# A macaron step on one core: the second product's sevenfold order starts with a one-block product, and stores follow their sums by a step

## The chip, the cores and the metric

The kernel runs on one core of a Trainium2 chip. The metric is the device time of one execution in microseconds. Its engines are TensorE (PE in the profile, with its weight loads as PEld), VectorE (DVE), ScalarE (ACT), GpSimd (POOL) and the sync engine (SP), which here issues all transfers (DMA). Each engine works through its own queue in program order; semaphores tie the queues together.

## The reference

One layer of a decoder: a half-step SwiGLU feed-forward block, a token mixer (a causal pooling branch and a Mamba-2 SSD branch under sigmoid gates), a second half-step feed-forward block, and a final norm, over 1024 prompt tokens and 64 sample tokens, in float32. The change touches the feed-forward blocks, in `after1` and `turn_x` the first one alone:

```python
D_MODEL = 1024; D_FF = 2816

def rmsnorm(x, g):
    return x * rsqrt(mean(x * x, -1) + EPS) * g

def swiglu(x, w_in, w_out):
    gu = x @ w_in
    g, u = gu[..., :D_FF], gu[..., D_FF:]
    return (silu(g) * u) @ w_out

x = x + 0.5 * swiglu(rmsnorm(x, norm_ffn1), ffn1_w_in, ffn1_w_out)
x = x + token_mixing(rmsnorm(x, norm_mix), ...)
x = x + 0.5 * swiglu(rmsnorm(x, norm_ffn2), ffn2_w_in, ffn2_w_out)
y = rmsnorm(x, norm_final)
```

## The kernel before

**Stages.** The first feed-forward block takes about 0 to 838 us of the span, the mixer 838 to 2190, the second feed-forward block 2190 to 2959. Activations lie features by tokens, in blocks of 128 features; the tokens are cut into halves of 512 and 576 (the second half has the 64 sample tokens).

**Precision.** Each matrix operand is split into a high and a low part, and each product takes three matmuls: high by high, high by low, low by high. ScalarE makes the high part (a copy that rounds), VectorE or GpSimd the low part by subtraction. For weights these are `wh` and `wl`, for the operands of the second product `hh` and `hr`.

**The first product of a block** makes the 22 hidden blocks of 128 (`ff` = 0 to 21). It, too, goes mostly by seven block products instead of eight (`wino`). A finished hidden block goes to `produced`. Two hidden blocks and two halves of the tokens (even and odd block, "e" and "o"; first and second half, 0 and 1) are the four quarters from which the second product by sevens takes its operands. There are 11 such pairs, `kk` = 0 to 10. The operands of products "2" and "5" are quarters as they stand, and `produced` stores them; those of "6", "7", "1", "4" and "3" are sums or differences, which `sums(kk)` makes on GpSimd and stores to device memory (`xq`), five stores of 128 x 544 per pair, one right behind each sum. The tiles come from one pool, `fx`, of 17 buffers, which the evictions of the first product, the input copy and the split of later weights use as well.

**The second product**, `second()`, runs seven products in the order of `ORDER2`. Each goes through two passes (`m0` = 0 and 2: four output tiles at a time, in four PSUM banks) of six groups of up to two pairs `kk`, 24 matmuls to a full group, 264 to a product. `second_weights` loads the weight blocks of a group (256 KB each) into one of six raw buffers; where the product has two blocks in `BLOCKS2`, GpSimd adds or subtracts them into `ws`; ScalarE then makes `wh`, VectorE `wl`. Products "3" and "4" have one block and need no sum. `fetch_x` loads the next product's 11 operands back ahead of time and splits them: the low part is made by GpSimd for "3" and "6" (`LO_POOL`), by VectorE for the others. For the products in `IN_PAIRS` the operands lie in a set of pair buffers that would be free otherwise. The residual (what is added to) is loaded by `residual` during the first product, and after each pass `add` accumulates the PSUM banks into it with VectorE. When the first half of the tokens has had its last contribution, `after(0, ...)` runs; for the first block that is `after1`, which starts the mixer's norm (`norm_parts`, a chain that makes one of 8 feature blocks, splits it and spills it at each step) and stores the residual back (`xspill`).

**What sets the order.** The instructions are emitted by a program with a clock of its own (`pe`), which each matmul advances by its ideal time. Side work is written as chains; a chain that yields a number is due again that many us of this clock later, and `tick()`, between groups of matmuls, steps the chains that are due. So `yield 4.0` between a load and its use puts about 4 us of matmuls between them in every queue. The order so written is the order of each engine's queue, SP's included: a store that waits for its sum holds every transfer behind it.

**The input copy.** In the first block a chain, `turn_x`, makes a transposed copy of the input for the residual: it loads 18 blocks of it (`xin`), yields, transposes each on TensorE (`ptr`), copies the results out of PSUM and stores them to `xspill`. Another chain, `part`, loads weights of later products, splits them (`ph`) and stores the parts.

Lines of the profile that are spoken of: 175 is every matmul, 179 every transpose; 321 to 328 load and store the parts, 367 and 369 split them; 455 and 456 split the first product's weights; 573, 577 and 579, 601, 609 and 613 evict it; 649 stores the operand of "5"; 672 to 687 are `sums` (674, 684 and 687 its stores); 738 to 749 `second_weights`; 764 to 766 `fetch_x`; 774 `residual`; 784 `add`; 900 the load of the input copy; 920 the norm.

Of the kernel before, what the change touches and what calls it, by code (L numbers as in the profile page):

```python
# [12 lines left out]
ALU = mybir.AluOpType  # L13
# [32 lines left out]
STEP_S = 1.0  # L46
POST, RIPE = 1.0, 3.0
GP = (1.5, 1.2)
HN_AT, HN_PACE = 3.0, 2.0
MP = 2.0  # L50
R_WAIT0 = 3.5
R_WAIT = 0.5
# [5 lines left out]
SETS = (((0,), (1,), (2,), (3,)), ((0, 1), (2,), (3,)))  # L58
PART_AT, PART_W, PART_PACE = 20.0, 4.0, 3.0
NKK, NQ, NA = NFF // 2, 272, 32  # L60
ORDER2 = "2517436"
BLOCKS2 = {"1": ((0, 0), (1, 1)), "2": ((0, 1), (1, 1)), "3": ((0, 0),), "4": ((1, 1),), "5": ((0, 0), (1, 0)),
           "6": ((0, 1), (0, 0)), "7": ((1, 0), (1, 1))}
MINUS2 = "67"
INTO2 = {"1": ((0, 0, 1), (1, 1, 1)), "2": ((1, 0, 1), (1, 1, -1)), "3": ((0, 1, 1), (1, 1, 1)),
         "4": ((0, 0, 1), (1, 0, 1)), "5": ((0, 0, -1), (0, 1, 1)), "6": ((1, 1, 1),), "7": ((0, 0, 1),)}
IN_PAIRS = "214"
LO_POOL = "36"
X_AT, X_PACE = 5.0, 2.2
SUM_PACE = 1.5  # L70
# [3 lines left out]
def tile_hybrid_pool_ssd_macaron(  # L74
# [88 lines left out]
    def finish(c):  # L163
        while not c.done:
            c.step()
# [491 lines left out]
    def sums(kk):  # L657

        t = {}
        for i in range(2):  # L660
            for h in HALVES:
                g = made.pop((2 * kk + i, h))
                if g is None:
                    g = fx(name="gr")
                    dma(g[:, : NTOK[h]], hdram[h][2 * kk + i])
                    yield 2.0
                t[i, h] = g
        e0, e1, o0, o1 = t[0, 0], t[0, 1], t[1, 0], t[1, 1]
        a, s, b0, b1, n = slice(0, 512), slice(512, 512 + NA), slice(NA, NA + 512), slice(NA + 512, 2 * NA + 512), 2 * NQ

        def both(p, out, x0, x1, y, op):
            G.tensor_tensor(out[:, a], x0[:, a], y[:, b0], op=op)  # L672
            G.tensor_tensor(out[:, s], x1[:, :NA], y[:, b1], op=op)
            dma(xq[p][kk], out[:, :n])

        both("6", fx(name="s6"), e0, e1, e1, ALU.add)
        yield SUM_PACE
        both("7", fx(name="s7"), o0, o1, o1, ALU.add)
        yield SUM_PACE
        both("1", fx(name="s1"), e0, e1, o1, ALU.add)  # L680
        yield SUM_PACE
        G.tensor_tensor(o0[:, a], o0[:, a], e0[:, a], op=ALU.subtract)
        G.tensor_tensor(o0[:, s], o1[:, :NA], e1[:, :NA], op=ALU.subtract)
        dma(xq["4"][kk], o0[:, :n])
        yield SUM_PACE
        G.tensor_tensor(e1[:, NA : NA + n], e1[:, NA : NA + n], o1[:, NA : NA + n], op=ALU.subtract)
        dma(xq["3"][kk], e1[:, NA : NA + n])

    def operands(prep, plain):

# [61 lines left out]
    def second(wo, after, half):  # L752

        X, C = {p: [] for p in ORDER2}, {}
        n = 2 * NQ

        def fetch_x(p, kks, pace):
            for kk in kks:
                if p in IN_PAIRS and kk < N_PAIR:
                    a, t, _ = pair(576, "hp")  # L760
                    t = t.bitcast(F32)
                else:
                    t, a = act((P, 576), F32, "hr"), act((P, 576), F32R, "hh")
                dma(t[:, :n], xq[p][kk])
                S.activation(a[:, :n], t[:, :n], AF.Identity)  # L765
                (G if p in LO_POOL else V).tensor_tensor(t[:, :n].bitcast(F32R), t[:, :n], a[:, :n].bitcast(F32), op=ALU.subtract)  # L766
                X[p].append((a, t.bitcast(F32R)))
                yield pace

        def residual(ms):  # L770
            for m in ms:
                for h in HALVES:
                    C[m, h] = fx(name="x")
                    dma(C[m, h][:, : NTOK[h]], xspill[h][m])
                yield 1.0

        def add(pt, m, side, c, sign):
            if side:
                to = [(1, NA + NQ * c, 0, NQ)]
            else:  # L780
                to = [(0, 0, 0, NQ)] if c == 0 else [(0, NQ, 0, NQ - NA), (1, 0, NQ - NA, NA)]
            for h, at, of, w in to:
                o = C[m, h][:, at : at + w]
                V.scalar_tensor_tensor(o, pt[:, of : of + w], 0.5 * sign, o, op0=ALU.mult, op1=ALU.add)  # L784

        finish(start(fetch_x(ORDER2[0], range(NKK - 1), 0.0)))
        ahead = start(fetch_x(ORDER2[0], range(NKK - 1, NKK), 0.0))
        for at, p in enumerate(ORDER2):
            finish(ahead)
            if at + 1 < len(ORDER2):  # L790
                last = at + 2 == len(ORDER2)
                ahead = start(fetch_x(ORDER2[at + 1], range(NKK), 1.6 if last else X_PACE), 14.0 if last else X_AT)
            for m0 in (0, 2):
                pts = [[psum("pd", "po") for _ in range(2)] for _ in range(2)]
                for kp in range(0, NKK, 2):
                    n2 = min(2, NKK - kp)
                    W2 = second_weights(wo, p, kp, n2, m0)
                    for j in range(2):
                        for k in range(n2):
                            xh, xl = X[p][kp + k]  # L800
                            for i, (w, x) in enumerate(((0, xh), (0, xl), (1, xh))):
                                for c in range(2):
                                    mm(pts[j][c][:, :NQ], W2[w][:, k, j * P : (j + 1) * P], x[:, c * NQ : (c + 1) * NQ],
                                       start=kp + k == 0 and i == 0, stop=kp + k == NKK - 1 and i == 2)
                            tick()
                    if at == 0 and kp == 2:
                        while summing:
                            finish(summing.pop())
                        res = start(residual(range(4, KD) if m0 == 0 else range(4)))
                if at == 0:  # L810
                    finish(res)
                with tc.high_priority(HP_EV):
                    for j in range(2):
                        for c in range(2):
                            for y, side, sign in INTO2[p]:
                                add(pts[j][c], 4 * y + m0 + j, side, c, sign)
            if p == "4":
                after(0, [C[m, 0] for m in range(KD)])
            if p == "3" and half:
                half(1, [C[m, 1] for m in range(KD)])  # L820
        after(1, [C[m, 1] for m in range(KD)])
# [72 lines left out]
    def turn_x(h):  # L894

        for q in range(2):
            x = [fx(name="xr") for _ in range(4)]
            for src, c0, c in blocks_of(h):
                t = fx(name="xin2")
                dma(t[:c, :512], src[:, q * 512 : (q + 1) * 512])  # L900
                yield 4.0
                pt = psum("ps", "ptr")
                for k in range(4):
                    tr(pt[:, k * P : k * P + c], t[:c, k * P : (k + 1) * P], ident[:c, :c])
# [6 lines left out]
    def norm_parts(xt, h, gi, out, pace=1.0, away=None):  # L911
# [5 lines left out]
        for k in range(KD):  # L917
# [5 lines left out]
            lo.append(b)  # L923
            xn.append(x)
            hl.append(both)
            if away:
                dma(away[k], x[:, :N])
            yield pace
        out.append((h, hi, lo, xn, hl))

    wi1 = ffn1_w_in[0]
# [2 lines left out]
    def after1(h, xt):  # L934
        o = []
        if h == 0:
            prep1m[0] = start(norm_parts(xt, 0, i_gm, o, HN_PACE, xnd), HN_AT), o
        for m in range(KD):
            dma(xspill[h][m], xt[m][:, : NTOK[h]])
        if h == 1:  # L940
            finish(prep1m[0][0])
            _, hi, lo, _, hl = prep1m[0][1][0]
# [963 lines left out]
```

## Time and profile before

| | before |
|---|---|
| median of 3 runs | 2959.21 us (2957.44 to 2970.2) |
| the profiled execution's own time | 2961.17 us |
| its span | 2958.9 us |
| granted TensorE clock, mean | 0.980 |
| TensorE matmuls busy | 2804.2 us, 95% |
| VectorE, ScalarE, GpSimd busy | 63%, 47%, 48% |
| transfers | 539.48 MB, mean 182 GB/s |

How rows are read. In a list of waits, "PE po L175 <- ACT wh L748: 24.7, 5, 10.7" says that TensorE, about to write `po` at line 175, waited for ScalarE's `wh` of line 748: 24.7 us in total, five times, the longest 10.7. In a group, "x60 | 81.5, 1361 | 80.2 <-..." is the count, the busy time in us, the mean of one in ns, and the engine's idle time ahead of the group with what ended it. In a stretch of time, "132.00:148.00 16.00, 9.93 (x55) ... 0.79 0.78 255" is the window and its length, busy us and count of TensorE's matmuls, its weight loads, VectorE, ScalarE and GpSimd, then the granted TensorE clock as a share of the full one, the share of the transfer engines that was busy, and GB/s. In a timeline a row is start, duration, engine, line and what it writes and reads; "[4.96 <-DMA xin...]" is how long the engine stood idle ahead of it and what ended that. Consecutive like rows are drawn together ("x10", with the busy time of all).

### The profile page before, as it was taken

To read this page: it belongs to the slowest core of one execution; us is meant where nothing else is said; L and a number is where in the kernel's file an instruction comes from. 1 tells how busy PE (TensorE), PEld (TensorE's weight loads), DVE (VectorE), ACT (ScalarE), POOL (GpSimd) and SP (SyncE) were. 2 spreads that over 40 slices of the span, in tenths; PEclk is the share of its full clock that TensorE was granted. 3 is DMA by queue.
4 is the path that set the end of the run, shared out by engine and by line. 5 is a ranking of instruction groups with operands and counts; after the bars stand their busy time and mean duration, and the time that the engine had idled before them with its cause. 6 is when DMAs were issued, how large, how long until landed. Compare 5 with 4: busy or idle time off the path is not lost. (4 is left out here: it accounts for less than half of the span.)

```text
span 2958.9 us, 54612 instructions
## 1 busy us (share of the span) xinstructions
PE 2804.2 (95%) x19834; PEld 2623.6 (89%) x19834; DVE 1869.3 (63%) x2916; ACT 1394.9 (47%) x3070; POOL 1429.9 (48%) x1450
## 2 busy tenths in 40 slices
PE   7989899799999999999999999799999999998997
PEld 6878899799979999999997887577999999987997
DVE  6645555676685386867676777866665554566853
ACT  5434344434354465555555667476233444443443
POOL 5455666654452264645542243323235766674524
PEclk9999999999999999999999999899999999998999
DMA  4666543597654555453358677686775332348845
GB/s 123 188 198 217 166 137 100 195 307 229 200 173 145 168 161 186 162 171 126 104 177 259 190 232 244 222 264 197 231 248 171 107 107 91 101 133 275 284 140 162
DMA packets 515790, 539.48 MB, mean 182 GB/s; under 512 B 41780, under 2 KB 356008, under 8 KB 515512
## 3 DMA queue, kind: packets, MB, share of 16 engines
q1 hardware_dynamic: 515504, 535.99, 56.7%
q8 instruction: 156, 2.56, 0.4%
q14 instruction: 114, 0.93, 0.1%
q10 hardware_dynamic: 16, 0.00, 0.0%
HBM read 383.43 MB, written 152.65 MB: 181 GB/s over the span
## 5 line engine op out<-in xcount | busy, mean ns | idle before, releaser
L175 PE MATMUL pw<-X,wh 128*128 128x288 f32 (+2 forms) x2832 | 630.7, 311 | 6.0 <-ACT v L573 2.4
L175 PEld LDWEIGHTS pw<-X,wh 128*128 128x128 f32 x2832 | 464.8, 191 | 29.0 <-ACT v L573 2.9
L175 PE MATMUL pw<-X,wl 128*128 128x288 f32 (+1 forms) x1644 | 475.8, 289 | 3.0 <-DVE wl L456 3.0
L456 DVE TENSOR_TENSOR wl<-s,wh 128x512 fp32r<-128x512 f32 x288 | 248.4, 864 | 268.5 <-ACT wh L455 250.4
L175 PE MATMUL pw<-hl,wh 128*128 128x256 f32 (+1 forms) x1536 | 394.0, 329 | 5.8 <-DVE t L579 5.1
L449 POOL TENSOR_TENSOR s<-wraw,wraw 128x512 f32<-128x512 f32 x144 | 203.0, 1409 | 307.0 <-DVE wl L456 208.5
L175 PE MATMUL pw<-hi,wh 128*128 128x288 f32 x1120 | 333.2, 297 | 3.0 <-DVE t L613 3.0
L175 PE MATMUL pw<-hi,wl 128*128 128x288 f32 x1120 | 331.5, 296 | 0.6 <-DVE wl L456 0.6
L175 PE MATMUL pw<-lo,wh 128*128 128x288 f32 x1120 | 331.6, 296 | 0.0
L175 PEld LDWEIGHTS pw<-X,wl 128*128 128x128 f32 x1644 | 313.9, 191 | 3.7 <-DVE wl L456 3.7
L175 PE MATMUL pw<-hl,wl 128*128 128x256 f32 x1072 | 301.5, 281 | 0.0
L175 PEld LDWEIGHTS pw<-hl,wh 128*128 128x128 f32 x1536 | 260.0, 190 | 27.8 <-DVE t L579 5.8
L456 DVE TENSOR_TENSOR wl<-wraw,wh 128x512 fp32r<-128x512 f32 x216 | 179.6, 832 | 120.1 <-ACT wh L455 116.9
L455 ACT ACTIVATE wh<-s 128x512 fp32r<-128x512 f32 x288 | 180.9, 629 | 148.3 <-PE pw L175 123.5
L744 POOL TENSOR_TENSOR ws<-wraw,wraw 128x512 f32<-128x512 f32 x120 | 165.7, 1384 | 166.9 <-DMA wraw<-in_ffn_w_out_dram 103.8
L175 PEld LDWEIGHTS pw<-hi,wh 128*128 128x128 f32 x1120 | 212.6, 190 | 9.5 <-DVE t L613 3.3
L175 PE MATMUL po<-hh,wh 128*128 128x272 f32 x848 | 184.8, 298 | 31.4 <-ACT wh L748 22.1
L175 PEld LDWEIGHTS pw<-hi,wl 128*128 128x128 f32 x1120 | 212.0, 189 | 1.1 <-DVE wl L456 1.1
L175 PEld LDWEIGHTS pw<-lo,wh 128*128 128x128 f32 x1120 | 212.6, 190 | 0.0
L175 PEld LDWEIGHTS pw<-hl,wl 128*128 128x128 f32 x1072 | 204.1, 190 | 0.0
L455 ACT ACTIVATE wh<-wraw 128x512 fp32r<-128x512 f32 x216 | 135.3, 627 | 138.9 <-PE pw L175 115.0
L175 PE MATMUL po<-hr,wh 128*128 128x272 f32 x848 | 180.4, 294 | 6.6 <-POOL hr L766 6.6
(401 smaller groups left out, 6869.5 us busy)
## 6 DMA issues: line engine op xcount, KB each, us to landing
wraw<-in_ffn_w_out_dram SPq DMA_DIRECT2D x240, 256.0 KB
wraw<-in_ffn_w_in_dram SPq DMA_DIRECT2D x188, 256.0 KB
wraw<-in_w_in_dram SPq DMA_DIRECT2D x144, 256.0 KB
wh<-part SPq DMA_DIRECT2D x116, 256.0 KB
wl<-part SPq DMA_DIRECT2D x116, 256.0 KB
hr<-xq SPq DMA_DIRECT2D x106, 272.0 KB
xq<-s SPq DMA_DIRECT2D x66, 272.0 KB
xq<-g SPq DMA_DIRECT2D x62, 272.0 KB
```

Source lines behind the costliest of these rows:

```text
L175: T.matmul(out, lhsT, rhs, start=start, stop=stop, skip_group_check=free)
L449: G.tensor_tensor(t, a, b, op=op)
L455: S.activation(wh, a, AF.Copy)
L456: V.tensor_tensor(wl, a, wh.bitcast(F32), op=ALU.subtract)
L744: G.tensor_tensor(s, raws[0], raws[1], op=ALU.subtract if p in MINUS2 else ALU.add)
```

## The change

Seven edits.

1. `ORDER2` turns from 2, 5, 1, 7, 4, 3, 6 into 4, 2, 5, 1, 7, 3, 6, and `IN_PAIRS` from "214" to "457": again the first, third and fifth product use the pair buffers. Product "7" is now the last that adds to the first half of the tokens, so `after(0, ...)` runs behind it, after the fifth product as before.
2. The eleventh operand of the first product, which depends on the last sums, is fetched behind the second group of weights, once those sums have been written into the queues, instead of ahead of the loop.
3. The residual blocks are loaded in the order in which the passes evict into them: 0, 4, 1, 5 and then 2, 6, 3, 7, instead of 4 to 7 and then 0 to 3.
4. The prefetch of the second product's operands starts 8.0 instead of 5.0 into the first.
5. `sums` makes the operands in the order 7, 4, 6, 1, 3 instead of 6, 7, 1, 4, 3, and keeps one store back: each is issued a step behind its sum, the last two steps carry stores alone.
6. `turn_x` yields 7.0 instead of 4.0 between a load and its transposes.
7. The mixer's first norm takes 3.2 instead of 2.0 per step, its spills are issued a step behind, and the stores of the residual become a chain that starts 5.0 later and issues one each 2.0, instead of eight at once.

```diff
-HN_AT, HN_PACE = 3.0, 2.0
+HN_AT, HN_PACE = 3.0, 3.2
-ORDER2 = "2517436"
+ORDER2 = "4251736"
-IN_PAIRS = "214"
+IN_PAIRS = "457"
...
# sums(kk)
+        late_ = []
...
-            dma(xq[p][kk], out[:, :n])
-
-        both("6", fx(name="s6"), e0, e1, e1, ALU.add)
-        yield SUM_PACE
+            late_.append((xq[p][kk], out[:, :n]))
+
+        def keep():
+            while len(late_) > 1:
+                dma(*late_.pop(0))
+
         both("7", fx(name="s7"), o0, o1, o1, ALU.add)
-        yield SUM_PACE
-        both("1", fx(name="s1"), e0, e1, o1, ALU.add)
         yield SUM_PACE
         G.tensor_tensor(o0[:, a], o0[:, a], e0[:, a], op=ALU.subtract)
         G.tensor_tensor(o0[:, s], o1[:, :NA], e1[:, :NA], op=ALU.subtract)
-        dma(xq["4"][kk], o0[:, :n])
+        late_.append((xq["4"][kk], o0[:, :n]))
         yield SUM_PACE
+        keep()
+        both("6", fx(name="s6"), e0, e1, e1, ALU.add)
+        yield SUM_PACE
+        keep()
+        both("1", fx(name="s1"), e0, e1, o1, ALU.add)
+        yield SUM_PACE
+        keep()
         G.tensor_tensor(e1[:, NA : NA + n], e1[:, NA : NA + n], o1[:, NA : NA + n], op=ALU.subtract)
-        dma(xq["3"][kk], e1[:, NA : NA + n])
+        late_.append((xq["3"][kk], e1[:, NA : NA + n]))
+        yield SUM_PACE
+        keep()
+        yield SUM_PACE
+        dma(*late_.pop(0))
...
# second()
         finish(start(fetch_x(ORDER2[0], range(NKK - 1), 0.0)))
-        ahead = start(fetch_x(ORDER2[0], range(NKK - 1, NKK), 0.0))
+        ahead = None
         for at, p in enumerate(ORDER2):
-            finish(ahead)
+            if ahead:
+                finish(ahead)
             if at + 1 < len(ORDER2):
                 last = at + 2 == len(ORDER2)
-                ahead = start(fetch_x(ORDER2[at + 1], range(NKK), 1.6 if last else X_PACE), 14.0 if last else X_AT)
+                ahead = start(fetch_x(ORDER2[at + 1], range(NKK), 1.6 if last else X_PACE), 14.0 if last else X_AT if at else 8.0)
...
                         while summing:
                             finish(summing.pop())
-                        res = start(residual(range(4, KD) if m0 == 0 else range(4)))
+                        if m0 == 0:
+                            finish(start(fetch_x(p, range(NKK - 1, NKK), 0.0)))
+                        res = start(residual((0, 4, 1, 5) if m0 == 0 else (2, 6, 3, 7)))
...
-            if p == "4":
+            if p == "7":
                 after(0, [C[m, 0] for m in range(KD)])
...
# turn_x(h)
-                yield 4.0
+                yield 7.0
...
# norm_parts(...)
+            yield pace
             if away:
                 dma(away[k], x[:, :N])
-            yield pace
...
# after1(h, xt)
-        for m in range(KD):
-            dma(xspill[h][m], xt[m][:, : NTOK[h]])
+
+        def away():
+            for m in range(KD):
+                dma(xspill[h][m], xt[m][:, : NTOK[h]])
+                yield 2.0
+
+        start(away(), 5.0)
```

The change moves instructions between queues. At the start of the second product (second feed-forward block), the sync engine's queue has the weight loads (`wraw`), the stores of the last sums (`xq7_10` is the store of the operand of product "7", pair 10) and the loads of the residual (`x`). A piece of it before:

```order
L738 DMA wraw_5700_32172<-in_ffn2_w_out_dram 128x2x256
L649 DMA xq5_10_295<-g_5626_31819 128x544
L674 DMA xq7_10_317<-s7_5674_32048 128x544
L674 DMA xq1_10_306<-s1_5677_32069 128x544
L684 DMA xq4_10_328<-g_5597_31693 128x544
L687 DMA xq3_10_339<-g_5566_31472 128x544
L774 DMA x_5683_32094<-xspill0_4_87 128x512
L774 DMA x_5684_32096<-xspill1_4_95 128x576
...
L764 DMA hr_5698_32167<-xq5_2_287 128x544
L738 DMA wraw_5701_32174<-in_ffn2_w_out_dram 128x2x256
```

Six more residual loads (`x`, blocks 5 to 7 of both halves) are left out at the dots. The same piece now:

```order
L750 DMA wraw_5690_32151<-in_ffn2_w_out_dram 128x2x256
L750 DMA wraw_5695_32186<-in_ffn2_w_out_dram 128x256
L750 DMA wraw_5702_32220<-in_ffn2_w_out_dram 128x2x256
L750 DMA wraw_5707_32255<-in_ffn2_w_out_dram 128x2x256
L649 DMA xq5_10_306<-g_5626_31819 128x544
L679 DMA xq7_10_328<-s7_5664_32007 128x544
L679 DMA xq4_10_284<-g_5597_31693 128x544
L679 DMA xq6_10_350<-s6_5668_32049 128x544
L679 DMA xq1_10_317<-s1_5669_32053 128x544
L699 DMA xq3_10_339<-g_5566_31472 128x544
L776 DMA hr_5670_32060<-xq4_10_284 128x544
L786 DMA x_5675_32077<-xspill0_0_83 128x512
```

Before, all stores and the pass's eight residual loads stood between one weight load and the next. Now eight weight loads stand ahead of the stores, all six of the first pass and two of the second (the last four are shown; the one of 128x256 ends the first pass), the eleventh operand's load (`hr`) right behind them, and the residual loads behind that.

The sync engine's queue around a load of the sample tokens in the input copy (`xin2`), before:

```order
L674 DMA xq7_2_309<-s7_447_2504 128x544
L684 DMA xq4_2_320<-g_379_2174 128x544
L687 DMA xq3_2_331<-g_322_1896 128x544
L900 DMA xin2_455_2546<-in_x_sample_dram 64x512
L674 DMA xq1_2_298<-s1_454_2542 128x544
L327 DMA part_458_2564<-ph_456_2561 128x512
L328 DMA part_460_2565<-pr_448_2508 128x512
L321 DMA pr_466_2610<-in_ffn2_w_in_dram 128x4x128
```

and now:

```order
L679 DMA xq6_3_343<-s6_550_3034 128x544
L679 DMA xq1_3_310<-s1_555_3067 128x544
L699 DMA xq3_3_332<-g_424_2414 128x544
L327 DMA part_563_3114<-ph_561_3111 128x512
L328 DMA part_565_3115<-pr_551_3050 128x512
L915 DMA xin2_569_3149<-in_x_sample_dram 64x512
L321 DMA pr_570_3166<-in_w_o_dram 128x4x128
L475 DMA wraw_632_3478<-in_ffn1_w_in_dram 128x4x128
```

Three stores of sums of one `sums` chain stood right ahead of that load; now two stores of weight parts do, and the sums' stores stand ahead of those.

GpSimd's queue in the fifth product of the second block, where "ws" is a sum of weight blocks and "hr" the low part of an operand for product "3". Before, from the end of product "7" into product "4":

```order
L744 TENSOR_TENSOR ws_5990_33690<-wraw_5988_33686,wraw_5989_33688 128x512
L744 TENSOR_TENSOR ws_5996_33728<-wraw_5994_33724,wraw_5995_33726 128x512
L744 TENSOR_TENSOR ws_6002_33766<-wraw_6000_33762,wraw_6001_33764 128x512
L744 TENSOR_TENSOR ws_6008_33804<-wraw_6006_33800,wraw_6007_33802 128x512
L744 TENSOR_TENSOR ws_6015_33843<-wraw_6013_33839,wraw_6014_33841 128x256
L766 TENSOR_TENSOR hr_6032_33941<-hr_6032_33941,hh_6033_33942 128x544
L766 TENSOR_TENSOR hr_6037_33976<-hr_6037_33976,hh_6038_33977 128x544
L766 TENSOR_TENSOR hr_6042_34011<-hr_6042_34011,hh_6043_34012 128x544
L766 TENSOR_TENSOR hr_6047_34046<-hr_6047_34046,hh_6048_34047 128x544
```

and now, from product "1" into product "7":

```order
L756 TENSOR_TENSOR ws_6004_33849<-wraw_6002_33845,wraw_6003_33847 128x512
L756 TENSOR_TENSOR ws_6009_33883<-wraw_6007_33879,wraw_6008_33881 128x512
L778 TENSOR_TENSOR hr_6012_33913<-hr_6012_33913,hh_6013_33914 128x544
L756 TENSOR_TENSOR ws_6016_33922<-wraw_6014_33918,wraw_6015_33920 128x512
L778 TENSOR_TENSOR hr_6019_33952<-hr_6019_33952,hh_6020_33953 128x544
L756 TENSOR_TENSOR ws_6023_33961<-wraw_6021_33957,wraw_6022_33959 128x512
L778 TENSOR_TENSOR hr_6026_33991<-hr_6026_33991,hh_6027_33992 128x544
L778 TENSOR_TENSOR hr_6033_34030<-hr_6033_34030,hh_6034_34031 128x544
L756 TENSOR_TENSOR ws_6030_34000<-wraw_6028_33996,wraw_6029_33998 128x512
L778 TENSOR_TENSOR hr_6049_34089<-hr_6049_34089,hh_6050_34090 128x544
L756 TENSOR_TENSOR ws_6037_34039<-wraw_6035_34035,wraw_6036_34037 128x256
```

The low parts stood by themselves; they stand between the weight sums of "7" now.

## The prediction

> **What bounds the kernel now.** I read the page first, then the list of what TensorE waited for, then stretches of time, then the queues behind the longest waits.
>
> ```profile
> PE 2804.2 (95%) x19834; PEld 2623.6 (89%) x19834; DVE 1869.3 (63%) x2916; ACT 1394.9 (47%) x3070; POOL 1429.9 (48%) x1450
> ...
> PE po L175 <- ACT wh L748: 24.7, 5, 10.7
> ...
> PE ptr L179 <- DMA xin<-in_x_prompt_dram: 10.6, 3, 6.1
> PE ptr L179 <- DMA xin<-in_x_sample_dram: 7.5, 2, 5.0
> PE po L175 <- DVE x L784: 10.1, 15, 3.1
> PE po L175 <- POOL hr L766: 6.6, 6, 1.7
> ```
>
> TensorE is busy 95% of the span, and the change takes no matrix product away, so only its waits and its half-clock stretches can be won. The rows give total us, times and the longest. Two places stand out: the second product waits for its weights (24.7 us in five waits, one of about ten in each feed-forward block), and the transposes of the input copy wait for their loads (18.1 us in five waits). The change edits code at both, and at the end of the first block's second product.
>
> **The change part by part.** The work per product stays the same: 264 matmuls, the same loads and stores. What moves is when.
>
> *The input copy (first block, 86 to 261 us).* Each row below is a stretch: length, busy time and count by engine, the granted clock, DMA.
>
> ```profile
> 132.00:148.00 16.00, 9.93 (x55) 9.09 (x54) 7.04 (x13) 4.13 (x9) 7.24 (x9) 0.79 0.78 255
> 148.00:164.00 16.00, 16.00 (x111) 15.06 (x109) 6.30 (x11) 6.17 (x15) 13.15 (x14) 1.00 0.49 162
> 164.00:172.00 8.00, 4.45 (x24) 4.04 (x23) 3.84 (x6) 2.48 (x5) 2.56 (x3) 0.79 0.92 275
> 204.00:228.00 24.00, 19.05 (x114) 17.59 (x113) 11.61 (x19) 8.02 (x21) 16.50 (x17) 0.86 0.68 231
> 252.00:268.00 16.00, 13.45 (x81) 12.27 (x80) 7.84 (x13) 5.60 (x14) 14.56 (x15) 0.89 0.43 152
> ```
>
> The undisturbed stretch runs 111 matmuls in 16 us, 6.94 per us. Against that the others lack 56, 31.5, 52.5 and 30, together 170 matmuls or 24.5 us. The waits themselves are 18.1 us; the rest is work at the lower clock after them. Why the loads are late shows in the sync engine's own order:
>
> ```profile
> 212.75 0.32 SPq L684 DMA_DIRECT2D xq<-g  x1
> 213.12 0.42 SPq L687 DMA_DIRECT2D xq<-g  x1
> 213.64 0.53 SPq L900 DMA_DIRECT2D xin<-in_x_sample_dram  x1
> ...
> 216.34 0.69 PE L179 MATMUL ptr<-ident,xin 64*128 64x64 f32 x4 [4.96 <-DMA xin<-in_x_sample_dram]
> ...
> SPq L674 <- POOL s L673: 96.4, 30, 6.6
> ```
>
> The load is issued 0.1 us after a store that itself waited for a GpSimd sum, and TensorE takes it 2.7 us later. From 80 to 540 us the queue spent 96.4 us in 30 such waits. The change does two things here. The gap between a load and its transposes grows by 3.0 us on the planner's clock (4.0 to 7.0). And each store is issued a step behind its sum, so that the queue reaches it when the sum is done; in the order after, the first sample load stands behind weight-part stores instead of three stores of sums. If only the 3.0 us came, the waits of 6.1, 5.0 and 2.6 us would shrink to 3.1, 2.0 and 0, and 3.6 to 0.6. I take 18 of the 24.5 us as won; the ends are 0 (other loads become the late ones) and 24.5.
>
> The same queueing holds the side work that splits later weights:
>
> ```profile
> 315.69 0.32 SPq L674 DMA_DIRECT2D xq<-s  x1
> 316.06 0.43 SPq L321 DMA_DIRECT2D pr<-in_w_o_dram  x1
> ...
> 319.12 0.63 ACT L367 ACTIVATE ph<-pr 128x512 fp32r<-128x512 f32 x1 [6.28 <-DMA pr<-in_w_o_dram]
> ...
> 321.19 0.80 PE L175 MATMUL pw<-hl,wh 128*128 128x512 f32 x1 [4.15 <-DVE t L579]
> ...
> 316.00:324.00 8.00, 3.85 (x17) 3.24 (x17) 3.62 (x6) 1.20 (x3) 2.37 (x3) 0.81 0.85 265
> ```
>
> A store waits for its sum, the load behind it is late, ScalarE waits for the load, VectorE for ScalarE, and an eviction stands behind both: 17 matmuls instead of 55.5, or 5.5 us. With the store later I take 4 us; the ends are 0 and 5.5.
>
> *The start of the second product (both blocks).* The second block's:
>
> ```profile
> 2672.35 1.19 PE po L175 x10
> ...
> 2681.99 1.32 POOL g L686
> ...
> 2683.70 4.57 SPq L774 DMA_DIRECT2D x<-xspill  x8
> ...
> 2689.07 1.74 SPq L738 DMA_DIRECT2D wraw<-in_ffn_w_out_dram  x3
> ...
> 2697.43 0.82 PE L175 MATMUL po<-hh,wh 128*128 128x272 f32 x2 [10.75 <-ACT wh L748]
> ...
> 2696.00:2704.00 8.00, 6.57 (x30) 6.57 (x31) 4.08 (x5) 3.52 (x6) 4.12 (x4) 0.53 0.75 233
> 2704.00:2714.00 10.00, 10.00 (x82) 10.00 (x81) 6.90 (x16) 3.13 (x5) 2.58 (x2) 1.00 1.07 379
> ```
>
> Product "2" starts at 2672.35. The fourth pair of weight blocks is issued only at 2689.07, behind the stores of the last sums (done at 2683.3) and eight residual loads (4.6 us of issuing). TensorE stands 10.75 us, then runs 30 matmuls in 6.57 us where the full rate of 8.2 per us gives 54: another 2.9 us. Both blocks together lose 24.7 + 2 x 2.9 = 30.5 us.
>
> After, product "4" comes first. It takes one weight block, no GpSimd sum, and 256 KB instead of 512 KB per step, so the six raw buffers hold its whole first pass: eight weight loads stand ahead of the stores. What is late next is its last operand. "4" needs a sum over the last two hidden blocks; "2" needed none. TensorE runs five steps, 120 matmuls or 14.6 us, to 2687.0. The five sums end at about 2684.8: the chain above has them done at 2683.3 with one weight sum among them, and one sum that was done early now comes after. The load of the eleventh operand stands behind six stores, so it goes out at 2685.2. A load of this kind on the quoted queue takes about 3.7 us and ScalarE and VectorE about 1.5 us more: ready at 2690.5. So TensorE stands 3.5 us, runs some 2 us behind at the lower clock, waits 1 us for evictions (the residual is loaded in order of use, so that is all) and perhaps 1.5 us for DMA: the transfers, 379 GB/s when full, are still queued then. That is 8 us against 15.2, and 2 x 7 = 14, of which I take 13. The ends: 0, if the store and the load back take as long as the weights did, and 30 less two short waits, 26.
>
> Rule beside row: the Trainium skill, TensorE: Matmul & The Clock Gate, "What's actually happening", says that one idle window of about 3.4 us halves the clock and about 3.4 us of work restores it. By that the 3.5 us wait costs 1.7 us rather than 2, and shorter waits none: 0.6 us in the sum. The trace does not agree on the short ones; the stretch 2905 to 2923, quoted next, is granted 0.91 with no wait there over 1.7 us.
>
> *Products "7", "3" and "6".* "4" used to stand fifth. "7" now does, and it has two weight blocks to sum while GpSimd also makes the low parts for "3".
>
> ```profile
> L744 POOL TENSOR_TENSOR ws<-wraw,wraw 128x512 f32<-128x512 f32 (+1 forms) x60 | 81.5, 1361 | 80.2 <-DMA wraw<-in_ffn_w_out_dram 47.1 <-DVE wl L749 24.5 <-DVE hr L766 3.5
> L766 POOL TENSOR_TENSOR hr<-hr,hh 128x544 fp32r<-128x544 f32 x22 | 31.1, 1417 | 23.9 <-ACT hh L765 22.5 <-PE po L175 0.9 <-DMA wraw<-in_ffn_w_out_dram 0.4
> ...
> L749 DVE TENSOR_TENSOR wl<-wraw,wh 128x512 fp32r<-128x512 f32 (+1 forms) x24 | 16.6, 701 | 28.9 <-ACT wh L748 26.5 <-DMA wraw<-in_ffn_w_out_dram 2.3
> ...
> 2905.00:2923.00 18.00, 13.47 (x86) 12.37 (x85) 5.16 (x6) 6.42 (x13) 14.86 (x12) 0.91 0.77 228
> 2923.00:2941.00 18.00, 17.98 (x143) 17.58 (x142) 6.37 (x12) 5.33 (x12) 2.03 (x2) 1.00 0.01 2
> ```
>
> 12 x 1.361 + 11 x 1.417 = 31.9 us of GpSimd in a product of 264 / 8.2 = 32.2 us: full. Product "6" has that mix today and lacks 57 of 143 matmuls between 2905 and 2923, 7.2 us. Unlike there, the sums of "7" run ahead through four buffers, and "3" has none, so lag is made up. I take 2 us per block, 4 in all; the ends are 0 and 14.
>
> *The end of the first block's second product.*
>
> ```profile
> 792.00:804.00 12.00, 8.63 (x54) 8.05 (x53) 10.46 (x17) 5.75 (x10) 7.56 (x6) 0.86 0.95 324
> 808.00:822.00 14.00, 10.12 (x72) 8.97 (x71) 13.30 (x15) 5.38 (x10) 9.78 (x7) 1.00 0.67 228
> ...
> L369 DVE TENSOR_TENSOR hl<-xn,hl 128x512 fp32r<-128x512 f32 x8 | 10.0, 1269 | 3.0 <-ACT hl L367 3.0
> L920 DVE SCALAR_TENSOR_TENSOR xn<-x,cols,r 128x512 f32<-128x512 f32 x8 | 8.9, 1136 | 0.0
> ```
>
> At 8.2 per us these two lack 44 and 43 matmuls, 10.6 us. The norm's 18.9 us on VectorE now spread over 8 x 3.2 us, later, mostly inside "6". That thins the first stretch and thickens the second. I take 2 us won; the ends are 4 lost and 8 won. Its stores now come a step later, behind fewer weight loads; the residual's spill is paced through "3", and for the second half through the mixer's first plain products, where its buffers are not the next ones wanted. The other edits (first fetch at 8.0, pair buffers for the first, third and fifth product as before) I cost at nothing: "2" is wanted 32 us after the start, so 24 us of product "4" cover the later fetch; without that cover they cost the 3 us of the delay.
>
> **The sum.** 18 + 4 + 13 - 4 + 2 = 33 us. The profiled execution took 2961.17 us, its span 2958.9; less 33 that is 2928.2. The median of the runs shown is 2.0 us lower, so I predict 2926 us.
>
> **The rivals.**
>
> *The copy's waits only move.* For it: 30 store waits remain in some form, and thirteen of the eighteen loads show no wait today and could. Against it: four of the five waits follow a store of a sum directly. Without the 22 us of the first two terms: 2948.
>
> *GpSimd and VectorE take turns in "7".* If no two of their two-operand operations overlapped, 31.9 us and 12 x 0.701 = 8.4 us would stand in line, 40.3 against 32.2: 8 us lost per block, 12 more than I took: 2938. For it: the full GpSimd; against it: "3" gives slack. The Trainium skill, SBUF — State Buffer, "Who interferes with whom", gives the rule: a VectorE operation with two inputs in SBUF blocks a GpSimd one that reads SBUF. The trace agrees in kind: beside the low parts of "6" on GpSimd, the norm's quoted split took 1269 ns, where the quoted split of a one-block weight, a two-input subtraction of the same size, took 701.
>
> *Late stores run the buffer pool dry* (slower). Each operand tile is held a step longer, and the copy holds four more of the 17 for half as long again. Then an eviction waits for a tile, and TensorE for its bank. Ten groups of sums per block, 20 in all: from 1.7 us per group on, the kernel is slower than before. At the 4.15 us of the quoted eviction wait in three groups of four, 62 us: 2988. Against it: 3 us is little beside a group's 42 us or so.
>
> *Everything is hidden.* The start's wait falls under the transfers, and the copy never waits: 2 x 6.5 + 6.5 more, 2907.
>
> **How the numbers follow.** Forecast 0.48, waits move 0.15, turns in "7" 0.15, pool dry 0.08, all hidden 0.14. Half a per cent, 15 us, is what this measurement can tell from no change: faster means under 2944, slower over 2974. The forecast and the last case are faster, and so is most of the third; the first rival is within, the pool mostly slower: 0.73, 0.20, 0.07. The range runs from 2905, all hidden, to 2952, past the waits that move; it leaves the pool and the edges out.
>
> **What would show it.** In the profile after: transposes that wait under 6 us in all; stores that wait far less than 96 us; at each start one wait of 2 to 5 us for an operand instead of ten for weights; GpSimd full in "7" with short waits. I am wrong if the start still costs ten, now for the eleventh operand, or if the ACT evictions of the first products wait for tiles.

## The result, and the profile after

| | before | changed |
|---|---|---|
| median | 2960.81 us (2957.44 to 2970.2, 4 runs) | 2922.19 us (2919.05 to 2928.26, 4 runs) |
| ratio | | 0.9867, interval 0.9839 to 0.9895 |
| profiled execution's own time, its span | 2961.17, 2958.9 us | 2928.26, 2925.9 us |
| granted clock, mean | 0.980 | 0.986 |

Faster by 38.6 us on the medians, by 33.0 us between the spans of the two profiled executions; the one of the changed kernel is 6.1 us above its median. The prediction was 2926 us, so the sum came out. Its terms did not, as the following shows.

The first row of the page and the list of what TensorE waited for, in the changed kernel:

```profile
PE 2797.0 (96%) x19834; PEld 2614.9 (89%) x19834; DVE 1855.2 (63%) x2916; ACT 1395.2 (48%) x3070; POOL 1418.2 (48%) x1450
```

```profile
PE po L175 <- DVE x L796: 25.0, 22, 4.6
...
PE po L175 <- DVE wl L761: 5.4, 7, 1.4
PE pw L175 <- DVE t L579: 5.0, 4, 2.2
...
PE po L175 <- POOL hr L778: 4.3, 6, 1.1
```

Two rows of before are gone: the transposes of the input copy (`ptr`, 18.1 us) wait for no load, and the second product's waits for its high weight parts fell from 24.7 us to 1.5. A row has grown in their place: TensorE waits 25.0 us for evictions of the second product (`x` at the line that was 784 and is 796), 10.1 before.

Where the time went, from the starts of the first and last matmul of each stretch in TensorE's timeline (first products are counted from the 2.1 us wait for `wl` that both kernels have at about 70 us):

| stretch | before | changed | difference |
|---|---|---|---|
| to the wait at 70 us | 73.1 | 69.3 | -3.8 |
| first product, first block | 492.0 | 465.1 | -26.9 |
| second product, first block | 270.7 | 266.3 | -4.5 |
| mixer | 1358.9 | 1363.9 | +5.0 |
| first product, second block | 477.4 | 475.3 | -2.1 |
| second product, second block | 270.7 | 269.9 | -0.7 |
| tail | 16.0 | 16.1 | 0.0 |

Of the 33 us, 27 come from the first block's first product, where the input is copied. The first row is unchanged code: over the profiled executions told of below it takes 69.3 to 73.3 us, whatever the kernel. The mixer, which no edit but the seventh touches, takes 1355.8 to 1361.4 us in all of them but two, and 1363.9 in this one.

The two second products, product by product (264 matmuls to a product, 1848 in all; the trace has every one of them, and a product lasts until the next one's first matmul). The stretches of time shown further down begin and end up to 1.8 us beside these boundaries; the 43.5 and 46.0 us for "7" in the expectations come from such stretches:

| product | block 1 before | changed | block 2 before | changed |
|---|---|---|---|---|
| "4" and "2" | 83.4 | 73.5 | 83.0 | 74.6 |
| "5" | 34.3 | 33.4 | 34.4 | 33.7 |
| "1" | 34.7 | 40.2 | 37.8 | 36.3 |
| "7" | 36.4 | 43.3 | 34.6 | 45.7 |
| "3" and "6" | 82.1 | 76.1 | 81.1 | 79.9 |

The start won 9.9 and 8.4 us. "7" gave back 6.8 and 11.1. Here is "7" of the second block as one stretch of time, before, with two of the waits in it:

```profile
2794.20:2829.17 34.97, 34.28 (x269) 33.89 (x268) 22.53 (x39) 14.81 (x27) 16.42 (x13) 1.00 0.68 216
```

```profile
ACT hh L765 <- DMA hr<-xq: 11.2, 6, 2.9
```

```profile
SPq L738 <- POOL ws L744: 9.9, 7, 2.1
```

and changed, with the longest waits of the engines in the same stretch behind it:

```profile
2785.78:2831.76 45.98, 38.36 (x268) 36.66 (x267) 18.30 (x35) 11.61 (x20) 19.52 (x16) 0.89 0.45 140
```

```profile
DVE wl L761 <- ACT wh L760: 27.7, 10, 4.6
ACT hh L777 <- DMA hr<-xq: 20.5, 7, 4.7
...
PE po L175 <- DVE x L796: 5.1, 3, 4.5
```

```profile
SPq L750 <- POOL ws L756: 19.7, 7, 4.0
```

The reader should see that no engine is busy: GpSimd works 19.5 of 46 us, VectorE 18.3, and the transfers are at 0.45. Everything waits for something. Of the time lost, TensorE's own waits are 7.6 us; the rest is work at the lower clock, 0.89 in this stretch. The timeline of the changed kernel shows for what:

```profile
2800.43 4.87 SPq L750 DMA_DIRECT2D wraw<-in_ffn_w_out_dram  x3
...
2803.09 1.29 POOL L756 TENSOR_TENSOR ws<-wraw,wraw 128x512 f32<-128x512 f32 x1 [0.36 <-DVE wl L761]
...
2805.41 0.41 SPq L776 DMA_DIRECT2D hr<-xq  x1
...
2809.03 0.66 ACT L777 ACTIVATE hh<-hr 128x544 fp32r<-128x544 f32 x1 [4.69 <-DMA hr<-xq]
2809.59 1.13 ACT L760 ACTIVATE wh<-ws 128x512 fp32r<-128x512 f32 x2
2809.76 1.33 POOL L778 TENSOR_TENSOR hr<-hr,hh 128x544 fp32r<-128x544 f32 x1 [2.17 <-ACT hh L777]
2810.24 1.40 DVE L761 TENSOR_TENSOR wl<-ws,wh 128x512 fp32r<-128x512 f32 x1 [4.01 <-ACT wh L760]
2811.57 1.60 DVE L796 SCALAR_TENSOR_TENSOR x<-po,x 128x272 f32<-128x272 f32 x6
```

Read it from the top. The second of the sync engine's three weight loads needs a raw buffer, and that comes free with GpSimd's sum, done at 2804.4. Only then, at 2805.41, goes out the load of an operand for "3". ScalarE waits 4.69 us for it, and the next weights' high part stands behind that in its queue; VectorE waits 4.01 us for the high part, and the evictions of the finished pass stand behind that in its own. TensorE waits 4.50 us for the evictions. GpSimd's next low part has waited for ScalarE too, and the sums that free the next raw buffers stand behind it. So the chain closes on itself: a ring through four queues in which each member waits for the one ahead. Nothing of it is there with "4" in fifth place, since a one-block product needs no sum: in "4" of the second block before, the sync engine waits for no weight sum at all, and ScalarE waits 1.6 us for operands.

"1" of the first block took 5.5 us more, for which the prediction has no term. TensorE waits 4.4 us for evictions there. In the profiles below of kernels with the same order of products it takes between 36.4 and 39.6 us, so part of this is the one execution; the rest was not followed up.

### The profile page after: what moved, and what is told of

Read it like the earlier page. It is cut to its first block, busy times and chain, and to the rows that moved or that the text cites. A ratio compares the mean times of both kernels' runs of the same rounds, so it can differ in the third digit from the quotient of the medians.

```text
span 2925.9 us, 54651 instructions
## 1 busy us (share of the span) xinstructions
PE 2797.0 (96%) x19834; PEld 2614.9 (89%) x19834; DVE 1855.2 (63%) x2916; ACT 1395.2 (48%) x3070; POOL 1418.2 (48%) x1450
## 5 line engine op out<-in xcount | busy, mean ns | idle before, releaser
L456 DVE TENSOR_TENSOR wl<-s,wh 128x512 fp32r<-128x512 f32 x288 | 240.3, 836 | 253.4 <-ACT wh L455 236.4
L449 POOL TENSOR_TENSOR s<-wraw,wraw 128x512 f32<-128x512 f32 x144 | 195.6, 1359 | 332.2 <-DVE wl L456 240.3
```

Source lines behind the costliest of these rows:

```text
L449: G.tensor_tensor(t, a, b, op=op)
L456: V.tensor_tensor(wl, a, wh.bitcast(F32), op=ALU.subtract)
```

## The experiments

Each time below is compared with runs of the kernel before on the same chip, as a ratio with its interval.

**The order alone.** Edits 1 to 4 on the kernel before:

```diff
-ORDER2 = "2517436"
+ORDER2 = "4251736"
-IN_PAIRS = "214"
+IN_PAIRS = "457"
...
+                        if m0 == 0:
+                            finish(start(fetch_x(p, range(NKK - 1, NKK), 0.0)))
+                        res = start(residual((0, 4, 1, 5) if m0 == 0 else (2, 6, 3, 7)))
...
+            if p == "7":
                 after(0, [C[m, 0] for m in range(KD)])
```

> Edits 1 to 4 alone (product order, late eleventh operand, residual in order of use, first prefetch at 8.0), on the kernel before. Theory A (from the two traces: the start of the second product wins about 10 us per block, and product "7", now beside the low parts of "3", gives back 7 to 11): start -20 us, product "7" +18 us, others about -3; in all -5 us, between -12 and +2, so about 2955. Theory B (the prediction's terms: -13 at the start, +4 in "7"): -9 us, about 2951, with "7" no longer than 37 us in either block.

Measured: 2964.32 us, 1.0016 (1.0006 to 1.0026), slightly slower. "7" of the second block took 44.5 us, with the same waits as in the changed kernel:

```profile
2825.15:2870.24 45.09, 37.78 (x271) 36.12 (x270) 17.74 (x35) 11.61 (x20) 19.44 (x16) 0.92 0.47 144
```

```profile
ACT hh L765 <- DMA hr<-xq: 19.5, 7, 4.4
```

```profile
PE pw L175 <- DVE t L579: 12.0, 5, 4.2
```

Both second products together were 3.8 us shorter (271.3 and 266.3 against 270.7 and 270.7), but both first products were longer (497.2 against 492.0, 481.3 against 477.4), with 12.0 us of eviction waits in place of 5.1. Theory B falls: the order is worth no 9 us. Theory A holds for its two large terms (18.6 us won at the start, 16.6 lost in "7") but misses the time, 4.8 us more where 2 was its upper end, because of the first products. They may pay for the operands of "4", ten of which are fetched ahead of the second product while the old `sums` makes them fourth of five; that was not tried apart.

**All but the order.** Edits 5, 6 and 7:

> Edits 5, 6 and 7 alone (sums in another order with stores a step late, the copy's load three us earlier, the norm wider and its spills paced), on the kernel before; complement of edits 1 to 4. Theory A: the 27 us that the first block's first product won, less up to 5 us at the mixer's start: -22 to -29 us, about 2934. Theory B (the prediction's terms: -22 for the copy, -2 for the end of the first block): -24 us, about 2936. Theory C (the copy's gain needs the new product order): less than 15 us won.

The edit, on the changed kernel, takes back what the diff above shows. Measured: 2922.16 us, 0.9877 (0.9861 to 0.9893). That is as much as the whole change gives, within the intervals. The first product of the first block took 465.5 us, as in the changed kernel; the transposes wait for no load.

**The copy's distance alone.**

```diff
# turn_x
-                yield 4.0
+                yield 7.0
```

> Edit 6 alone (7.0 instead of 4.0 between a load of the input copy and its transposes). Theory A (distance cures the waits): the five waits of the transposes, 18.1 us, shrink by 3.0 us each or to nothing, 12.6 us, and with them part of the half-clock stretches: -13 to -20 us, about 2943. Theory B (the queue behind the sums' stores is the cause, and the load only gets in line earlier): under 8 us won, the transposes still wait over 10 us in all.

Measured: 2950.02 us, 0.9969 (0.9959 to 0.9979), 9.5 us won. TensorE's waits between 80 and 570 us:

```profile
PE pw L175 <- DVE t L579: 8.7, 5, 2.6
PE pw L175 <- DVE t L613: 5.5, 2, 4.0
PE ptr L179 <- DMA xin<-in_x_prompt_dram: 3.1, 1, 3.1
```

It lies between the two theories. The transposes' waits fell from 18.1 to 3.1 us, more than theory A asked, but the first product only from 492.0 to 484.1. The waits went to the evictions: the side work that splits weights is still held by stores that wait for their sums, and evictions stand behind that work. From 80 to 540 us the sync engine waits 91.9 us for sums, 96.4 before; ScalarE's waits for the loads of weight parts (`ph`) are 35.6 us in all up to 570 us, 36.9 before and 21.9 in the changed kernel.

**The late stores alone.** The whole of edit 5, so the sums are made in their new order too; its core:

```diff
# sums
...
+            late_.append((xq[p][kk], out[:, :n]))
+
+        def keep():
+            while len(late_) > 1:
+                dma(*late_.pop(0))
...
```

> Edit 5 alone (sums in the order 7, 4, 6, 1, 3, each store issued a step behind its sum). Theory A (each of edits 5 and 6 carries a part): -8 to -14 us, about 2949. Theory B (the queue is the cause): -18 to -27 us, about 2938, with the transposes' waits under 4 us in all. Theory C (the late stores only hold tiles longer): no gain or a loss of some us, with the sync engine's waits for GpSimd's sums still over 80 us between 80 and 540 us.

Measured: 2947.35 us, 0.9962 (0.9948 to 0.9976), 12 us won; the first product took 489.5 us. The transposes wait nearly as long as before, in more places:

```profile
PE ptr L179 <- DMA xin<-in_x_prompt_dram: 12.5, 6, 4.3
...
PE ptr L179 <- DMA xin<-in_x_sample_dram: 3.3, 1, 3.3
```

So theory B falls: with the queue freer (70.9 us of waits for sums from 80 to 540 us), 4 us of distance are still too few. Theory A's size holds, though in the profiled execution, which is 4.3 us above the median, the first product won only 2.5 us and the rest is spread.

**Both, without edit 7.**

> Edits 5 and 6 together, without edit 7, on the kernel before. Edit 6 alone gave 0.9969 of the time before, edit 5 alone 0.9962, together with edit 7 they gave 0.9877. Theory additive: 0.993 (about 2939), and the rest of the gain was edit 7's. Theory both needed (an early load still stands behind a store that waits, and a free queue still leaves too little distance): the first product of the first block falls from 492 to about 465 us as with all three, 0.989 to 0.991, about 2931, and edit 7 is worth the 6 us by which product "6" of the first block got shorter with it.

Measured: 2930.08 us, 0.9904 (0.9888 to 0.9919). The first product took 465.2 us: 26.8 won, where the two alone give 7.9 and 2.5. On the medians the two together win 28.5 us, alone 9.5 and 12.2. So each needs the other for a part of its worth, and the additive theory, 0.993, lies just outside the interval. Whether edit 7 is worth the rest is not settled: 0.9904 against 0.9877 speaks for some us, but the intervals overlap, and the two profiled spans, 2921.0 and 2920.1, are alike.

**Edit 7 undone** in the changed kernel:

> The changed kernel with edit 7 undone (norm at 2.0 per step, its spills and the residual's stores at once). Theory A (edit 7 thins the end of the second product but delays the side work at the mixer's start, where 3.8 us went): the mixer's start comes back to 2 us behind the last matrix product instead of 5.7, products "3" and "6" of the first block get 2 to 6 us longer: between -3 and +4 us, about 2923. Theory B (the wider norm is worth the 2 us of the prediction or more): +2 to +8 us, about 2926.

Measured: 2926.53 us, 0.9883 (0.9867 to 0.9899) against the changed kernel's 0.9867: the intervals overlap. In the profile the first block's second product took 271.1 us against 266.3, and the mixer 1356.9 against 1363.9. A part of the latter is one wait, which the kernel with edit 7 has right behind the last product and this one has not:

```profile
806.34 0.50 PE L175 MATMUL pdt<-hl,wl 128*128 128x512 f32 x1 [2.09 <-DVE wl L307]
```

In both pairs of profiles "3" and "6" of the first block are shorter with edit 7 (76.1 us against 81.9 here, 76.9 against 80.7 between all but the order and both without edit 7) and the mixer is longer. Both theories have a piece of it, and the sum is within what can be told.

**The low parts of "3" on VectorE**, in the changed kernel:

```diff
-LO_POOL = "36"
+LO_POOL = "6"
```

> The changed kernel with the low parts for product "3" made by VectorE instead of GpSimd. Theory ring (a weight load waits on the sync engine for GpSimd's sum of an earlier group, that sum stands behind a low part, the low part waits for ScalarE's high part, that one for an operand's load, and that load stands behind the weight load): the ring is opened, "7" falls from 43.5 and 46.0 us to 35 in each block, -15 to -20 us, about 2905. Theory taking turns (VectorE's and GpSimd's two-operand operations exclude each other): the work only changes engine, 12 x 1.36 + 12 x 0.7 + 11 x 0.7 = 32.4 us in line against 32.2: "7" falls to about 34 us as well. Both expect a gain here; rival: VectorE is the next bound, its evictions come late, and under 8 us are won.

Measured: 2906.20 us, 0.9820 (0.9805 to 0.9835), 16 us below the changed kernel and below both kernels of this case. "7" took 37.4 and 36.0 us; this is the second block's:

```profile
2774.91:2811.33 36.42, 34.31 (x269) 33.92 (x268) 19.14 (x39) 11.40 (x20) 8.06 (x7) 1.00 0.52 170
```

The sync engine's waits for weight sums fell from 19.7 us in this stretch to 8.7:

```profile
SPq L750 <- POOL ws L756: 8.7, 6, 3.3
```

This run tells the ring from VectorE as the next bound, but not from two engines that take turns. The next does.

**The loads of "3" from another queue**, all arithmetic left where it is:

```diff
-                dma(t[:, :n], xq[p][kk])
+                (nc.scalar.dma_start if p == "3" else dma)(t[:, :n], xq[p][kk])
```

> The changed kernel with the loads of the operands of product "3" issued by ScalarE's queue instead of the sync engine's. All work of GpSimd and VectorE stays as it is. Theory ring: the loads no longer stand behind weight loads that wait for GpSimd, so ScalarE's waits for them (20.5 us in seven waits in "7" of the second block) fall under 5 us and "7" comes back to 35 to 38 us: -12 to -18 us, about 2907. Theory taking turns, or GpSimd simply full: nothing changes in "7", 43 to 46 us, about 2922.

Measured: 2910.86 us, 0.9835 (0.9822 to 0.9849). "7" took 39.0 and 38.3 us, with as much GpSimd work in the stretch as the changed kernel has (19.1 us in 17 instructions there, 19.5 in 16):

```profile
2775.77:2814.61 38.84, 35.88 (x270) 35.46 (x269) 17.89 (x36) 12.72 (x22) 19.14 (x17) 0.96 0.59 176
```

```profile
ACT hh L777 <- DMA hr<-xq: 9.2, 6, 2.1
```

```profile
SPq L750 <- POOL ws L756: 15.9, 8, 3.1
```

The sync engine still waits 15.9 us for weight sums here, but no load of an operand of "3" stands behind them. ScalarE's waits fell from 20.5 us to 9.2, not under 5, and the gain of 11 us is a little under the 12 to 18 expected. Turns between the two engines would have left "7" as it was. The ring is shown as the cause of most of what "7" lost: of 6.8 and 11.1 us, 4.3 and 7.4 come back with this link taken away, 5.9 and 9.7 with the other. The Trainium skill, DMA: Bandwidth & Descriptors, "Issuing engines are not separate DMA queues", says that issuing from several engines saves only the time that the sequencer takes to issue. Here 22 loads of about 0.4 us of issue moved, and 11 us were won. Time of issue was not what bound the sync engine, which in the changed kernel stood waiting for 35 of the 46 us of "7" in the second block: what the second queue saves is the place behind a load that waits for a buffer.

**Both remedies at once.**

> The changed kernel with both remedies: low parts for "3" on VectorE and the loads of its operands on ScalarE's queue. Alone they gave 0.982 and 0.9835. Theory one ring (both open the same one): no more than 3 us below the better, 2903 to 2908. Theory two causes (the queue of loads, and the two engines' operations in each other's way): they add up, 2892 to 2898.

Measured: 2908.85 us, 0.9832 (0.9817 to 0.9846). Not additive, so the theory of two causes falls: one ring.

**The low parts of "6" on VectorE as well** (`LO_POOL = ""`).

> The changed kernel with the low parts for "3" and for "6" made by VectorE. Opening the ring in "7" gave 0.982 of the time before (2906). Theory ring in "6" too (it has two weight blocks, its operands' low parts are on GpSimd, its first pass takes 23 to 25 us instead of 16): "6" gets 4 to 7 us shorter in each block, about 2896. Rival: VectorE is loaded in "6" of the first block by the norm, and the operands of "6" come late for another reason (their loads start 14 us into "3"): within 3 us of 2906, or longer.

Measured: 2907.30 us, 0.9827 (0.9812 to 0.9841), no gain. The second products were shorter in the profile (257.1 and 258.8 us against 261.5 and 260.4 with the low parts of "3" alone on VectorE; "6" by 3.3 and 2.7), the mixer longer (1363.8 against 1359.6). The theory of a second ring in "6" has no support in the time.

**The residual's loads spread out**, with the low parts of "3" on VectorE:

```diff
# residual
-                yield 1.0
+                yield 2.5
```

> The changed kernel with low parts for "3" on VectorE, and the residual loads of the first product 2.5 apart instead of 1.0. With the low parts alone 2906. Theory transfers (the second pass of "4", 21 us instead of 16, waits because residual, operands and weights all want the transfer engines at once, which are full there): the wait for evictions and the half-clock stretch shrink, 2 to 4 us per block, about 2900. Rival (the residual then comes after the evictions want it, or its order in the queue does not matter): 2906 to 2912.

Measured: 2918.79 us, 0.9862 (0.9846 to 0.9877), 12 us slower than with the low parts alone. "2" behind it got longer (its first pass 22.6 us in the first block, 18.4 without), "4" did not get shorter. The loads want to be early; the theory of too many transfers at once falls.

## Why the prediction was right, and where its terms were wrong

The sum was 33 us in the profile, and 33.0 came by the spans; on the medians 38.6. That agreement is luck: the terms were off, and they cancel. The sizes below are each from one execution, and stretches of unchanged code differ by up to 4 us between executions.

**The input copy, 18 + 4: measured 26.9.** The mechanism was right, with both halves of it: distance and the stores behind their sums. The step that priced the distance alone was wrong, though. It shrank each wait by 3 us and took the time for won; with the distance alone the waits did shrink, to 3.1 us, and 7.9 us were won, since the side work stayed late and other waits took over. A wait that is gone is time won only if the next one behind it is gone too, which here took both edits.

Two signs named in advance bear this out. The transposes wait for no load, and the sync engine's waits for sums between 80 and 540 us fell, though not "far":

```profile
SPq L679 <- POOL s L674: 63.5, 25, 6.0
```

Against 96.4 us in 30 waits, so a step of the planner is often still too short for a sum to be done. Over the copy this is the stretch of 130 us, before and then changed:

```profile
134.00:264.00 130.00, 111.88 (x714) 104.23 (x715) 65.79 (x116) 51.08 (x125) 70.67 (x71) 0.93 0.66 214
```

```profile
130.00:260.00 130.00, 126.00 (x845) 117.29 (x844) 80.08 (x129) 58.00 (x139) 82.89 (x80) 1.00 0.69 224
```

131 matmuls more in the same time, 18.9 us at 6.94 per us, which is the 18 of the first term; the other 8 came later in the product, where 4 was taken.

**The start, 13: measured 18.4** (9.9 and 8.4 for "4" and "2" against the same two before). The pieces differ. The 3.5 us wait for the eleventh operand, which was also one of the signs, did not come: the last sum ended 10.0 us after the product's start, not 12.5, and the load went out the sooner. The residual's evictions cost more than 1 us: in the second block TensorE stood 2.84 us for them and then ran at little more than half its rate for 6 us, while the transfer engines were full. The evictions began at 2660.5, behind work of VectorE that had waited for an operand of "2". The row of that work, and the two stretches of 20 us:

```profile
2659.28 0.72 DVE L778 TENSOR_TENSOR hr<-hr,hh 128x544 fp32r<-128x544 f32 x1 [3.00 <-ACT hh L777]
```

```profile
2639.90:2659.90 20.00, 18.62 (x146) 18.24 (x144) 6.67 (x10) 4.59 (x9) 9.84 (x10) 1.00 0.68 236
2659.90:2679.90 20.00, 18.22 (x120) 17.94 (x121) 10.88 (x26) 6.67 (x11) 2.37 (x2) 0.83 1.07 369
```

**"7", 4: measured 18.** This is the step that failed, and its measured size lies outside the ends of 0 and 14. It said that the sums of "7" run ahead through four buffers, so that lag is made up. But the buffers that ran out were the six raw ones, and the loads of "3" stand in the same queue as the loads that wait for them. The sign named for it, a full GpSimd with short waits, did not come either: GpSimd worked 19.5 of 46 us, and the 31.9 us counted for it did not bound the product. The prediction looked at the load on an engine and not at who stands behind whom on the sync engine, although it had done just that for the copy. Of the rivals, turns between GpSimd and VectorE had nearly the size (8 us per block) and not the cause. Its 701 ns, set beside 1269 ns for 128x512, is a mean over 20 subtractions of 128x512 (725 ns) and four of half that size; the reading holds with 725 too.

**The end of the first block, 2: not settled.** "3" and "6" there took 6.0 us less, the mixer 5.0 more, and with edit 7 undone the time is the same within what can be measured.

By edits the picture is plainer still. The prediction gave the order and what belongs to it 9 us of gain (13 less 4); alone it is 0.16% slower, and the change without it is as fast as with it. The copy's two edits carry most of the gain. The rival that the waits only move is in part what the longer distance does alone; with the late stores alone the waits mostly stay, and together they go. Of the rival of late stores and a pool run dry nothing is seen: the waits for the eviction at line 613, 3.0 us before, are gone, and those at line 579 are 5.0 us against 5.1. Of the rival in which everything is hidden, 2907, the changed kernel is far. With the ring opened the time is 2906, but by another way: "4" and "2" still take 73.3 and 74.4 us there. That run is 16 us below all but the order, so with the ring opened the new order may well pay; the old order with the low parts of "3" on VectorE was not run.

## What to carry to other kernels

When a product moves beside another one's prefetch, follow the shared queues around once: a load that waits for a buffer, whose release stands behind an instruction that waits for a later load of the same queue, makes a ring, and no engine's busy share shows it. Two edits at one wait can be worth more together than the sum of each alone, here 28.5 us against 21.7, so undo them one at a time and also together before any is called useless. And a sum that comes out right says nothing of its terms: check each against its own stretch.

## What was not expected of the hardware

A wait of 2.84 us was followed by some 6 us at little more than half the rate. The groups of four matmuls that take 0.67 us otherwise take 1.11:

```profile
2661.36 0.59 PE L175 MATMUL po<-hp,wh 128*128 128x272 f32 x1 [2.84 <-DVE x L796]
...
2663.54 1.11 PE L175 MATMUL po<-hp,wh 128*128 128x272 f32 x4
...
2668.61 0.67 PE L175 MATMUL po<-hp,wh 128*128 128x272 f32 x4
```

The clock granted in that time is 0.50:

```profile
2661.40:2664.00 2.60, 2.28 (x9) 2.00 (x9) 2.60 (x11) 1.29 (x2) 0.00 (x0) 0.50 1.06 383
2664.00:2667.50 3.50, 3.50 (x17) 3.50 (x17) 1.61 (x3) 0.66 (x1) 0.00 (x0) 0.50 1.07 377
```

Over the 6 us this loses about 3, as much as the wait itself. The Trainium skill, TensorE: Matmul & The Clock Gate, "What's actually happening", halves the clock after one idle window of about 3.4 us, and by that this wait would cost only its own length; the trace does not agree, and the prediction's rows, by which short waits cost their share of the clock, were the better guide.
